# A hybrid decoder layer: attention scores of all parts one behind the other, the recurrence's 64x64 products over four quarters, normed rows turned by whole transposes

## The chip, the cores and the metric

The kernel runs on one core of one Trainium2 chip. The metric is the device time of one execution in microseconds, as the median of the runs. Before the change it is 431.32 us (three runs, 431.30 to 431.98). A core has engines that run side by side, each with its own queue of instructions in a fixed order: TensorE (PE, matrix products, with PEld for its weight loads), VectorE (DVE), ScalarE (ACT), GpSimd (POOL) and SyncE (SP, which here issues DMAs). An engine that waits for a semaphore holds up all that stands behind the waiting instruction in its queue.

## The reference

One layer of a decoder, for 256 tokens of width 1024, in float32. Two branches read the same normed input: RWKV-7 time mixing, which is a recurrence over tokens with a 64x64 state in each of 8 heads, and causal attention with 8 heads of 64. Their results are projected, gated, merged and projected again, and a gated MLP with a short convolution follows.

```python
h = rms_norm(x, norm1_g[l])
proj = h @ w_in[l]                       # one projection for both branches and the gates
...
y_a = rwkv7_time_mix(z_rwkv, ...)
...
y_b = moba_attention(q, k, v)
u_a = y_a @ w_branch_a[l]
u_b = y_b @ w_branch_b[l]
...
x = x + (g_a * u_a + g_b * u_b) @ w_out[l]
h2 = rms_norm(x, norm2_g[l])
x = x + conv_ffn(h2, w_ffn_up[l], ffn_conv_w[l], ffn_conv_b[l], w_ffn_down[l])
```

Inside the time mixing, for each head and token, then a norm over the 64 values of each head:

```python
def step(state, inp):
    r_t, w_t, k_t, v_t, a_t, b_t = inp
    sa = jnp.einsum('bhvk,bhk->bhv', state, a_t)
    state = (state * w_t[:, :, None, :] + sa[..., None] * b_t[:, :, None, :]
             + v_t[..., None] * k_t[:, :, None, :])
    return state, jnp.einsum('bhvk,bhk->bhv', state, r_t)
...
mu = jnp.mean(y, axis=-1, keepdims=True)
var = jnp.mean(jnp.square(y - mu), axis=-1, keepdims=True)
y = ((y - mu) * lax.rsqrt(var + GN_EPS)).reshape(B, S, C)
```

At this size the attention has one block of keys, so each query attends to all keys up to its own.

## The kernel before

**Weights.** Every large weight comes by DMA in pieces of 512 KB (`raw`, L221, issued on SP, four buffers), is split into a rounded part `whi` (a cast on ACT, L233) and the rest `wlo` (a subtraction on DVE, L243), and TensorE sums three products into `acc`: high by high (L271), low by high (L273), high by low (L276). L292, L293 and L296 do the same where the weight is the stationary operand. This is called the bulk here.

**Threads.** The middle of the kernel is written as generators: `chain` (the recurrence and its preparation), `bulk` (input projection, gates, the attention branch), `att` (attention) and a group norm for each chunk. Each hands back an estimate (cost, latency) with `yield`; a small loop uses the sum to choose which thread writes its next piece, so that bulk products stand between the dependent steps of the others. A scheduler then fixes the order of each engine. When the recurrence has ended, the branch of the recurrence (`branch(0)`, on `yah` and `yal`) follows, then w_out and the MLP.

**Recurrence.** The 256 tokens are cut into 4 chunks of 64. A head is given by its parity q, which is also the half of the partitions (0 to 63 or 64 to 127) that its operands lie in, and by ct (0 to 3). `pz0` (L665) is computed for all chunks ahead. Inside a chunk a triangular 64x64 matrix has to be inverted: 16x16 blocks on DVE, written to DRAM and read back into place in `X` by eight DMAs on SP (L643), then two steps on TensorE: `pp` (L711, X times the part of G below the diagonal), masked on DVE to `P` (L716), `px` (L727), added to X (L728). X has two sides, the inverse and its transpose. Then for each chunk: `pz` (L791, the state times AR; from the second chunk), added to Z (L793), `pu` (L798), copied to VU by ACT (L800) and DVE (L801), `pS` (L807) for the new state `Sn`, `pyt` in two parts that sum (L822 with the state, L826 with VU), copied to `yt`. The group norm of the chunk works on `yt` with tokens on partitions (`yc`, L758 to L767), turns it with eight 64x64 products against the identity (`pc`, L774), applies scale and bonus (`yf`, L776 and L777) and splits the result into `yah` (ACT, L778) and `yal` (DVE, L779).

**Attention.** q and k are turned (`pqk`, L876) and copied to `qkT` (ACT, L877). It has three parts: the first 128 queries with all heads, then the second 128 queries with four heads twice. For each, `scores` makes products `ps` (L893), masks or copies them into `sc` (DVE L896, ACT L899) and does the softmax (L902 to L909, exponentials on ACT), turns the weights with transposes (`ppt`, L918, copied to `pT`), and when a half of the queries is complete `weighted` makes `po` (L931), split into `ybh` (ACT, L935) and `ybl` (DVE, L936). The gates' tanh is `gt` (ACT, L955); a branch's product is merged with `gt` on DVE (L964).

PSUM has three pools: three banks `acc` for bulk, three `ch` for the recurrence, two `at` for attention.

The recurrence's loop asks for a half of the array with the operands' half of rows and of columns the same:

```python
pu = chp("pu").rearrange("p (a n) -> p a n", a=8)
for h in range(8):
    ct, q = divmod(h, 2)
    pe.matmul(pu[bsl(q), ct], X[bsl(q), 1, 4 * ct + c], Z[bsl(q), ct], start=True, stop=True)
```

Of the kernel before, what the change touches and what calls it, by code (L numbers as in the profile page):

```python
# [36 lines left out]
def body(tc, x, positions, norm1_g, w_in, rwkv_mu, w_decay_up, decay_bias, w_aaa_up,  # L37
# [5 lines left out]
    with ctx:  # L43
# [447 lines left out]
        def chain():  # L491
# [67 lines left out]
            KB = cst.tile([128, 2112], F32, name="KB")  # L559
# [45 lines left out]
            for g in range(2):  # L605
# [7 lines left out]
                for ct in (2 * g, 2 * g + 1):  # L613
                    for q in range(2):
                        dve.tensor_tensor(G[q][:, 4 * ct:4 * ct + 4], pg[ct % 2][q],
                                          gmask[:, None, :].to_broadcast([128, 4, 128]), op=OP.mult)
# [22 lines left out]
            pool.memset(X, 0.0)  # L639
            for q in range(2):  # L640
                for b in range(4):
                    q0 = bsl(q).start + 16 * b
                    nc.sync.dma_start(X[q0:q0 + 16, :, :, 16 * b:16 * b + 16],  # L643
                                      d2[4 * q + b].rearrange("x u (i n) -> i x u n", i=16))
# [15 lines left out]
            Z0 = b4("Z0", (128, 4, 4, 64))  # L660
            pz = [chp("pz0").rearrange("p (c a n) -> p c a n", c=2, a=4) for _ in range(2)]
            for c in range(4):
                for ct in range(4):
                    for q, hs in PAR:
                        pe.matmul(pz[c // 2][bsl(q), c % 2, ct], G[q][hs, 4 * ct + c, 0:64],  # L665
                                  VU[hs, c, q, ct], start=True, stop=True)
            for j in range(2):
                act.copy(Z0[:, 2 * j:2 * j + 2], pz[j])
            yield 2.5, 3.0
# [27 lines left out]
            def pair(t, g):  # L697
                return t.rearrange("p (a c) n -> p a c n", c=4)[:, :, 2 * g:2 * g + 2]


            us = [[(4 * ct + 2 * g + c, 2 * ct + c) for ct in range(4) for c in range(2)] for g in range(2)]

            def bank(nm):
                p = chp(nm)
                return p.rearrange("p (u n) -> p u n", u=8), p.rearrange("p (a c n) -> p a c n", a=4, c=2)

            def below(g):
                p, _ = bank("pp")
                for u, i in us[g]:
                    for q in range(2):  # L710
                        pe.matmul(p[bsl(q), i], G[q][bsl(q), u, 0:64], X[bsl(q), 0, u], start=True, stop=True)  # L711
# [7 lines left out]
            def onto(g, P, side):  # L719

                p, p4 = bank("px")
                for u, i in us[g]:
                    for q in range(2):
                        l, r = X[bsl(q), 1, u], P[bsl(q), i]
                        if side:
                            l, r = r, l
                        pe.matmul(p[bsl(q), i], l, r, start=True, stop=True)  # L727
                return lambda: dve.tensor_tensor(pair(X[:, side], g), pair(X[:, side], g), p4, op=OP.add)  # L728

            yield 0, 11.0  # L730
            pp = [below(g) for g in range(2)]
            P = [masked(pp[g], m16) for g in range(2)]
            yield 2.5, 3.5
            adds = [onto(0, P[0], 0), onto(1, P[1], 0), onto(0, P[0], 1)]
            for a in adds:
                a()
            yield 3.3, 4.5
            pp = [below(g) for g in range(2)]
            add = onto(1, P[1], 1)
            P = [masked(pp[g], m32) for g in range(2)]  # L740
            add()
            yield 3.3, 4.5
            for a in [onto(g, P[g], 1) for g in range(2)]:
                a()
# [6 lines left out]
            def group_norm():  # L751

                for c in range(4):
# [18 lines left out]
                    for ct in range(4):  # L772
                        for q, hs in PAR:
                            pe.matmul(p[hs, ct], yc[hs, ct], ident[hs, hs], start=True, stop=True)  # L774
# [10 lines left out]
            for c in range(4):  # L785
                Z = Z0[:, c]
                if St is not None:
                    pz = chp("pz").rearrange("p (a n) -> p a n", a=8)
                    for h in range(8):
                        ct, q = divmod(h, 2)  # L790
                        pe.matmul(pz[bsl(q), ct], AR[half(q), 4 * ct + c, 0], St[half(q), ct],  # L791
                                  start=True, stop=True)
                    dve.tensor_tensor(Z, pz[:, 0:4], Z, op=OP.add)  # L793
                    yield 0.8, 2.3
                pu = chp("pu").rearrange("p (a n) -> p a n", a=8)
                for h in range(8):
                    ct, q = divmod(h, 2)
                    pe.matmul(pu[bsl(q), ct], X[bsl(q), 1, 4 * ct + c], Z[bsl(q), ct],  # L798
                              start=True, stop=True)
# [383 lines left out]
```

## Time and profile before

| | us |
|---|---|
| median of 3 runs | 431.32 |
| the profiled execution | 431.12 |
| its span, first to last instruction | 429.0 |

The span is the time from the first to the last instruction; 2.12 us of the execution lie outside. A row of a group names line, engine, operation, out<-in, tile (rows*columns of the array), shape and count, then busy time in us and the mean of one in ns, then the idle time ahead. A row of the timeline gives start and length; a matmul's length overlaps the next one's, so what a burst costs TensorE is the distance from its start to the start of what follows. A window's row gives for each engine the busy time and the count, and the granted clock as a share of full speed.

| stage of the span | us |
|---|---|
| pz0 | 90.6 to 92.6 |
| first product on X (pp) | 117.2 |
| first scores (ps) | 123.7 |
| first pu of the recurrence | 147.9 |
| last pu of the recurrence | 183.0 |
| last weights turned (ppt), weighted (po) | 188.6, 190.5 |
| first product of the attention branch | 193.7 |
| last turned chunk (pc) | 194.1 |

### The profile page before, as it was taken

Reading aid. Unit: us, or ns where it says so; the run is one execution under the profiler, and the core shown is the slowest. Engines: PE = TensorE matmul, PEld = TensorE weight load, DVE = VectorE, ACT = ScalarE, POOL = GpSimd, SP = SyncE. Lnnn points to the kernel's source line nnn. Section 1 sums busy time; section 2 is a strip of 40 time slices with the busy share of each in tenths; the row PEclk is TensorE's granted clock in tenths of the full one; section 3 lists DMA queues with packets and bytes.
Section 4 is the critical chain, followed back from the end, with each engine's and each line's share of the span. In section 5 each row is a group of like instructions: output and inputs, shape, how many; then the busy total and the mean of one; then the engine's idle time right before and its main releaser. Section 6 shows DMA issues by size and latency. Waiting matters only on the chain.

```text
span 429.0 us, 8164 instructions
## 1 busy us (share of the span) xinstructions
PE 416.8 (97%) x3249; PEld 365.9 (85%) x3249; DVE 322.0 (75%) x553; ACT 239.1 (56%) x386; POOL 27.1 (6%) x47
## 2 busy tenths in 40 slices
PE   7799999999999999979999999999999999999996
PEld 3799989888899989969987878888888888888885
DVE  3797899779437567766786599888797797796783
ACT  6599645455345468793356466465464454464550
POOL 6920060000000000000000000000000000000000
PEclk9999999999999999989999999999999999999999
DMA  8776655563743534531665275656656656656622
GB/s 256 205 197 200 193 147 151 154 166 99 148 148 101 149 99 120 176 101 53 194 189 165 88 244 175 218 195 196 190 165 211 186 184 200 191 169 213 191 67 98
DMA packets 62404, 70.71 MB, mean 165 GB/s; under 512 B 9117, under 2 KB 52835, under 8 KB 62368
## 3 DMA queue, kind: packets, MB, share of 16 engines
q1 hardware_dynamic: 61664, 69.48, 54.3%
q0 software_dynamic: 688, 0.73, 0.6%
q8 instruction: 25, 0.41, 0.4%
q14 instruction: 11, 0.09, 0.1%
q10 hardware_dynamic: 16, 0.00, 0.0%
HBM read 68.76 MB, written 1.44 MB: 164 GB/s over the span
## 4 chain that ended last, share of the span: by engine, by line
PE 89%; ACT 4%; DVE 3%; DMA 2%; issue 1%; POOL 1%; SPq 0%; DVEq 0%; ACTq 0%; POOLq 0%
PE acc L1080 17%; PE acc L1083 8%; PE acc L271 8%; PE acc L276 8%; PE acc L273 8%; PE acc L292 4%; PE acc L293 4%; PE acc L296 4%; PE f L1099 4%; PE f L1098 4%; PE f L1100 4%; PE px L727 1%; DMA x<-in_x_dram 1%; DMA raw<-in_w_ffn_up_dram 1%; PE pp L711 1%; PE pgr L611 1%
## 5 line engine op out<-in xcount | busy, mean ns | idle before, releaser
L233 ACT CAST whi<-raw 128x1024 fp32r<-128x1024 f32 x121 | 126.7, 1051 | 124.4 <-PE acc L1080 44.9
L243 DVE TENSOR_TENSOR wlo<-raw,whi 128x1024 fp32r<-128x1024 f32 x124 | 152.2, 1230 | 50.6 <-PE acc L276 13.4
L1080 PE MATMUL acc<-hx,whi 128*128 128x512 f32 x352 | 96.7, 395 | 0.5 <-DVE bs L1088 0.5
L1080 PEld LDWEIGHTS acc<-hx,whi 128*128 128x128 f32 x352 | 60.1, 188 | 9.1 <-DVE bs L1088 1.0
L1083 PEld LDWEIGHTS acc<-hx,wlo 128*128 128x128 f32 x352 | 53.4, 188 | 7.9
L271 PE MATMUL acc<-hx,whi 128*128 128x256 f32 x232 | 58.4, 287 | 0.0
L273 PE MATMUL acc<-hx,whi 128*128 128x256 f32 x232 | 56.5, 279 | 0.0
L1083 PE MATMUL acc<-hx,wlo 128*128 128x256 f32 x352 | 54.6, 278 | 0.0
L271 PEld LDWEIGHTS acc<-hx,whi 128*128 128x128 f32 x232 | 43.7, 188 | 1.4 <-issue 0.5
L273 PEld LDWEIGHTS acc<-hx,whi 128*128 128x128 f32 x232 | 43.8, 189 | 0.4 <-issue 0.3
L276 PE MATMUL acc<-hx,wlo 128*128 128x256 f32 x232 | 36.1, 278 | 1.1 <-DVE wlo L243 1.1
L276 PEld LDWEIGHTS acc<-hx,wlo 128*128 128x128 f32 x232 | 30.9, 188 | 1.3 <-DVE wlo L243 1.3
L1099 PE MATMUL f<-whi,hb 128*128 128x512 f32 x80 | 31.2, 390 | 0.0
L1100 PE MATMUL f<-wlo,hb 128*128 128x512 f32 x80 | 31.2, 390 | 0.0
L1098 PE MATMUL f<-whi,hb 128*128 128x512 f32 x80 | 31.2, 389 | 0.0
L1088 DVE TENSOR_REDUCE an<-acc 128x256 f32<-128x512 f32 x22 | 15.2, 689 | 7.2 <-PE acc L1083 6.3
L292 PE MATMUL acc<-whi,hx 128*128 128x512 f32 x48 | 19.3, 402 | 0.0
L293 PE MATMUL acc<-whi,hx 128*128 128x512 f32 x48 | 18.8, 392 | 0.0
L1100 PEld LDWEIGHTS f<-wlo,hb 128*128 128x128 f32 x80 | 15.0, 188 | 3.2
L1098 PEld LDWEIGHTS f<-whi,hb 128*128 128x128 f32 x80 | 15.0, 188 | 2.8
L1099 PEld LDWEIGHTS f<-whi,hb 128*128 128x128 f32 x80 | 15.0, 188 | 2.7
L296 PE MATMUL acc<-wlo,hx 128*128 128x512 f32 x48 | 14.9, 392 | 0.0
(294 smaller groups left out, 650.5 us busy)
## 6 DMA issues: line engine op xcount, KB each, us to landing
raw<-in_w_ffn_up_dram SPq DMA_DIRECT2D x44, 512.0 KB, 4.5
raw<-in_w_in_dram SPq DMA_DIRECT2D x42, 512.0 KB, 4.6
raw<-in_w_ffn_down_dram SPq DMA_DIRECT2D x22, 512.0 KB, 4.1
raw<-in_w_out_dram SPq DMA_DIRECT2D x8, 512.0 KB, 3.7
x<-in_x_dram SPq DMA_DIRECT2D x8, 256.0 KB, 3.4
raw<-in_w_branch_b_dram SPq DMA_DIRECT2D x4, 512.0 KB, 4.3
raw<-in_w_branch_a_dram SPq DMA_DIRECT2D x4, 512.0 KB, 4.0
out_dram<-o SPq DMA_DIRECT2D x3, 256.0 KB, 2.0
```

The costliest lines, as they stand in the source:

```text
L233: act.copy(hi[:, :k * c], raw[:, :k * c])
L243: eng.tensor_tensor(lo[:, :n], raw[:, :n], hi[:, :n].bitcast(F32), op=OP.subtract)
L271: pe.matmul(om, wh[:, k, ms], xh[:, k0 + k], start=k0 + k + m == 0, stop=False, skip_group_check=True)
L273: pe.matmul(om, wh[:, k, ms], xl[:, k0 + k], start=False, stop=False, skip_group_check=True)
L276: pe.matmul(om, wl[:, k, ms], xh[:, k0 + k], start=False, stop=k0 + k == nk - 1 and m == n - 1, skip_group_check=True)
L292: pe.matmul(ps_[t], xh[:, K, ts], wh[:, k], start=K == 0, stop=False)
L293: pe.matmul(ps_[t], xl[:, K, ts], wh[:, k], start=False, stop=False)
L1080: pe.matmul(ps_[m], wh[:, k, ms], hx[:, k0 + k].rearrange("p a s -> p (a s)"), start=k0 + k == 0, stop=False, skip_group_check=True)
L1083: pe.matmul(ps_[m][:, 0:S], wl[:, k, ms], hh[:, k0 + k], start=False, stop=k0 + k == 7, skip_group_check=True)
L1098: pe.matmul(fin[f], hb[:, 0, i, ts], wh[:, 0, cs], start=st, stop=False)
L1099: pe.matmul(fin[f], hb[:, 1, i, ts], wh[:, 0, cs], start=False, stop=False)
L1100: pe.matmul(fin[f], hb[:, 0, i, ts], wl[:, 0, cs], start=False, stop=False)
```

## The change

1. Attention: the scores and the softmax of all three parts are written first, then the transposes and weighted products of all. For this the parts keep buffers of their own: `sc0`, and `sc1` in the place of `KB`, which is no longer read then.
2. The 64x64 products of pz0, pp, px, pz, pu and pyt are written in an order `QA` over two parities, so that they fall on all four quarters (half of rows, half of columns) of the array. Rows go by one parity and columns by the other, so each step writes two PSUM banks, one for each, in place of one; the copies behind it become twice as many with half the size. G's slots and Z0's layout follow. The transposed side of px (`turned_`) stays on two quarters.
3. `pc`: two transposes of 128x128 for a chunk in place of eight 64x64 products.
4. X is read back by more DMAs: eight for side 0 on SP, then sixteen for side 1, eight on SP and eight on POOL.
5. The estimates in `yield` change with it.

In the program as it is scheduled, three places are shown. In the first burst of `pp` (L724 now), all eight products on G of one parity stand ahead of the eight of the other; from there on they alternate in the order of QA.

ScalarE's queue around the copies `qkT` of the turned q and k, ahead of the first softmax, before:

```order
L842 COPY qkv<-acc 128x512
L877 COPY qkT_1521<-pqk 128x512 x2
L955 ACTIVATE gt<-acc 128x512
L877 COPY qkT_1564<-pqk 128x512 x2
L233 CAST whi<-raw 128x1024 x3
L906 ACTIVATE sc,sm<-sc,mx 128x128 x8
```

and now:

```order
L875 COPY qkv<-acc 128x512
L910 COPY qkT_1537<-pqk 128x512 x2
L233 CAST whi<-raw 128x1024
L910 COPY qkT_1580<-pqk 128x512
L1002 ACTIVATE gt<-acc 128x512
L233 CAST whi<-raw 128x1024
L910 COPY qkT_1580<-pqk 128x512
L233 CAST whi<-raw 128x1024
L943 ACTIVATE sc,sm<-sc,mx 128x128 x8
```

Two of the three casts of weights, which need their raw piece from DRAM, now stand between the copies.

TensorE's queue where the recurrence ends, before (pyt is that of the last chunk, pc turns the last chunk, L271 and L273 on ybh and ybl are the attention branch):

```order
L826 MATMUL pyt<-VU,G_784 64x64
L826 MATMUL pyt<-VU,G_785 64x64
L918 MATMUL ppt<-ident,sc 128x128 x8
L931 MATMUL po<-pT,qkv 64x128 x16
L271 MATMUL acc<-ybh,whi 128x256 x2
L774 MATMUL pc<-ident,yc 64x64 x8
L273 MATMUL acc<-ybl,whi 128x256
L271 MATMUL acc<-ybh,whi 128x256
```

and now at the last pc:

```order
L273 MATMUL acc<-ybl,whi 128x256
L276 MATMUL acc<-ybh,wlo 128x256 x4
L798 MATMUL pc<-ident,yc 128x128 x2
L271 MATMUL acc<-yah,whi 128x256 x3
L273 MATMUL acc<-yal,whi 128x256
L271 MATMUL acc<-yah,whi 128x256
L273 MATMUL acc<-yal,whi 128x256
```

The last transposes and weighted products of attention have moved ahead of the recurrence's last chunks, the attention branch stands ahead of the last pc, and the recurrence's branch (on yah and yal) directly behind it.

VectorE's queue at the same place, before:

```order
L767 TENSOR_TENSOR yc<-yc,st 128x256
L936 TENSOR_TENSOR ybl<-po,ybh 128x4x128
L776 TENSOR_TENSOR yf<-pc,A_1335 128x256
L777 TENSOR_TENSOR yf<-yf,zr 128x256
L779 TENSOR_TENSOR yal<-yf,yah 128x4x64
L964 SCALAR_TENSOR_TENSOR gt<-gt,acc 128x512
L243 TENSOR_TENSOR wlo<-raw,whi 128x1024
```

and now:

```order
L792 TENSOR_TENSOR yc<-yc,st 128x256
L1011 SCALAR_TENSOR_TENSOR gt<-gt,acc 128x512
L243 TENSOR_TENSOR wlo<-raw,whi 128x1024
L1011 SCALAR_TENSOR_TENSOR gt<-gt,acc 128x512
L801 TENSOR_TENSOR yf<-pc,A_1351 128x256
L243 TENSOR_TENSOR wlo<-raw,whi 128x1024
L802 TENSOR_TENSOR yf<-yf,zr 128x256
L804 TENSOR_TENSOR yal<-yf,yah 128x4x64
L1011 SCALAR_TENSOR_TENSOR gt<-gt,acc 128x512
```

The gates' merge and a split of weights now stand ahead of and between the two operations on the last chunk.

The diff, cut to its core:

```diff
+        QA = ((0, 0), (1, 1), (0, 1), (1, 0))
+        def gslot(ct, c=0):
+            return 8 * (ct % 2) + 4 * (ct // 2) + c
...
-            KB = cst.tile([128, 2112], F32, name="KB")
+            KB = cst.tile([128, 2112], F32, name="KB", tag="KB")
...
+            def to_x(eng, side, x, us_, src):
+                b = src[1]
+                q0 = bsl(side).start + 16 * b
+                eng.dma_start(X[q0:q0 + 16, x, us_, 16 * b:16 * b + 16],
+                              d2[4 * src[0] + b, x, src[2]].rearrange("u (i n) -> i u n", i=16))
             for q in range(2):
                 for b in range(4):
-                    q0 = bsl(q).start + 16 * b
-                    nc.sync.dma_start(X[q0:q0 + 16, :, :, 16 * b:16 * b + 16],
-                                      d2[4 * q + b].rearrange("x u (i n) -> i x u n", i=16))
+                    to_x(nc.sync, q, 0, slice(0, 16), (q, b, slice(0, 16)))
+            for q in range(2):
+                for b in range(4):
+                    for a in range(2):
+                        to_x((nc.sync, nc.gpsimd)[a], a, 1, slice(8 * q, 8 * q + 8), (q, b, slice(8 * a, 8 * a + 8)))
...
             for c in range(4):
-                for ct in range(4):
-                    for q, hs in PAR:
-                        pe.matmul(pz[c // 2][bsl(q), c % 2, ct], G[q][hs, 4 * ct + c, 0:64],
-                                  VU[hs, c, q, ct], start=True, stop=True)
+                for j in range(2):
+                    for q, a in QA:
+                        ct = 2 * j + a
+                        pe.matmul(pz[q][bsl(a), c, j], G[q][half(q), gslot(ct, c), 0:64],
+                                  VU[half(q), c, q, ct], start=True, stop=True)
...
+            def below():
+                p = [bank("pp") for _ in range(2)]
+                for i in range(8):
+                    for q, a in QA:
+                        u = 8 * a + i
+                        pe.matmul(p[q][bsl(a), i], G[q][bsl(q), u, 0:64], X[bsl(q), 0, u], start=True, stop=True)
                 return p
...
+            def plain(P):
+                p = [bank("px") for _ in range(2)]
+                for i in range(8):
+                    for q, a in QA:
+                        pe.matmul(p[a][bsl(q), i], X[bsl(a), 1, 8 * q + i], P[q][bsl(a), i], start=True, stop=True)
+                return p
+            def turned_(q, P):
+                p = bank("px")
+                for i in range(8):
+                    for a in range(2):
+                        pe.matmul(p[bsl(a), i], P[bsl(a), i], X[bsl(a), 1, 8 * q + i], start=True, stop=True)
+                return p
...
                     p = chp("pc").rearrange("p (a n) -> p a n", a=8)
-                    for ct in range(4):
-                        for q, hs in PAR:
-                            pe.matmul(p[hs, ct], yc[hs, ct], ident[hs, hs], start=True, stop=True)
+                    for j in range(2):
+                        pe.transpose(p[:, 2 * j:2 * j + 2].rearrange("p a n -> p (a n)"),
+                                     yc[:, 2 * j:2 * j + 2].rearrange("p q n -> p (q n)"), ident)
...
+                    pz = two("pz")
+                    for j in range(2):
+                        for q, a in QA:
+                            ct = 2 * j + a
+                            pe.matmul(pz[q][bsl(a), j], AR[half(q), 4 * ct + c, 0], St[half(q), ct],
+                                      start=True, stop=True)
+                    for q in range(2):
+                        dve.tensor_tensor(Z0[:, q, c], pz[q][:, 0:2], Z0[:, q, c], op=OP.add)
+                    yield 0.5, 2.3
+                pu = two("pu")
+                for j in range(2):
+                    for q, a in QA:
+                        pe.matmul(pu[a][bsl(q), j], X[bsl(a), 1, 8 * q + 4 * j + c], Z0[bsl(a), q, c, j],
                                   start=True, stop=True)
-                act.copy(VU[bsl(0), c, 0], pu[bsl(0), 0:4])
-                dve.tensor_copy(VU[bsl(1), c, 1], pu[bsl(1), 0:4])
-                yield 0.9, 2.3
+                for a in range(2):
+                    act.copy(VU[bsl(0), c, 0, a:4:2], pu[a][bsl(0), 0:2])
+                    dve.tensor_copy(VU[bsl(1), c, 1, a:4:2], pu[a][bsl(1), 0:2])
+                yield 0.6, 2.3
...
+                py = two("pyt")
...
+            sc0 = b4("sc", (128, 8, 128))
+            sc1 = cst.tile([128, 2112], F32, name="sc1", tag="KB")[:, 0:2048].rearrange("p (h k) -> p h k", k=256)
+            parts = ((0, 0, 8, sc0), (1, 0, 4, sc1[:, 0:4]), (1, 1, 4, sc1[:, 4:8]))
...
-            p0 = yield from scores(0, 0, 8)
-            yield weighted(0, p0)
-            pa = yield from scores(1, 0, 4)
-            pb = yield from scores(1, 1, 4)
-            yield weighted(1, pa + pb)
-            yield 0, 2.5
+            for i, part in enumerate(parts):
+                scores(*part)
+                yield 0.9, 3.0
+                softmax(*part)
+            yield 0, 4.0
...
+            p0 = turned_w(*parts[0])
+            yield 0.9, 2.5
+            weighted(0, p0)
+            pa = turned_w(*parts[1])
+            yield 1.8, 3.0
+            pb = turned_w(*parts[2])
+            yield 0.9, 2.5
+            weighted(1, pa + pb)
+            yield 1.9, 2.5
```

More of the change, by code (lines that the diff above doesn't have):

```diff
@@ L659, in chain @@
             yield 2.5, 4.0
[L660 to L661 removed]
+            Z0 = b4("Z0", (128, 2, 4, 2, 64))
+            pz = [chp("pz0").rearrange("p (c j n) -> p c j n", c=4, j=2) for _ in range(2)]
             for c in range(4):
[L663 to L669 removed]
+                for j in range(2):
[4 more added lines that the diff above has]
+            for q in range(2):
+                act.copy(Z0[:, q], pz[q])
+            yield 1.4, 3.0
             bp = zr
@@ L695, in chain @@
             A2 = bon
-            def pair(t, g):
-                return t.rearrange("p (a c) n -> p a c n", c=4)[:, :, 2 * g:2 * g + 2]
-            us = [[(4 * ct + 2 * g + c, 2 * ct + c) for ct in range(4) for c in range(2)] for g in range(2)]
             def bank(nm):
[L704 to L711, printed above, removed]
+                return chp(nm).rearrange("p (u n) -> p u n", u=8)
+            def below():
[4 more added lines that the diff above has]
+                        pe.matmul(p[q][bsl(a), i], G[q][bsl(q), u, 0:64], X[bsl(q), 0, u], start=True, stop=True)
                 return p
@@ L717, in masked @@
                 return P
[L719 to L728, printed above, removed]
-            yield 0, 11.0
@@ L731, in chain, with added @@
[L731 to L744, printed above, removed]
+            def added(side, g, p):
+                v = X[:, side, 8 * g:8 * g + 8]
+                dve.tensor_tensor(v, v, p, op=OP.add)
@@ new lines, in chain @@
+            yield 0, 11.0
+            pp = below()
+            P = [masked(pp[q], m16) for q in range(2)]
+            yield 1.4, 3.5
+            px = plain(P)
+            pt = turned_(0, P[0])
+            for a in range(2):
+                added(0, a, px[a])
+            added(1, 0, pt)
+            yield 2.4, 4.5
+            pp = below()
+            pt = turned_(1, P[1])
+            P = [masked(pp[q], m32) for q in range(2)]
+            added(1, 1, pt)
+            yield 2.4, 4.5
+            pt = [turned_(q, P[q]) for q in range(2)]
@@ L745, in chain @@
+            for q in range(2):
+                added(1, q, pt[q])
             yield 2.3, 4.0
@@ L815, in chain @@
                         dve.tensor_tensor(Sn, Sn, pcb, op=OP.mult)
-                py = chp("pyt").rearrange("p (a n) -> p a n", a=8)
+                py = two("pyt")
                 if St is not None:
-                    for h in range(8):
-                        ct, q = divmod(h, 2)
-                        hs = half(q)
-                        pe.matmul(py[hs, ct], AR[hs, 4 * ct + c, 1], St[hs, ct], start=ct == 0,
-                                  stop=False, skip_group_check=True)
-                for h in range(8):
-                    ct, q = divmod(h, 2)
-                    pe.matmul(py[half(q), ct], G[q][:, 4 * ct + c, 64:128], VU[:, c, q, ct],
-                              start=St is None and ct == 0, stop=ct == 3, skip_group_check=True)
+                    for j in range(2):
+                        for q, a in QA:
+                            ct = 2 * j + a
+                            pe.matmul(py[q][half(a), j], AR[half(q), 4 * ct + c, 1], St[half(q), ct],
+                                      start=j == 0, stop=False, skip_group_check=True)
+                for j in range(2):
+                    for q, a in QA:
+                        ct = 2 * j + a
+                        pe.matmul(py[q][half(a), j], G[q][:, gslot(ct, c), 64:128], VU[:, c, q, ct],
+                                  start=St is None and j == 0, stop=j == 1, skip_group_check=True)
                 ny[c] = t1("yt", (128, 4, 64))
-                act.copy(ny[c], py[:, 0:4])
-                yield 1.9, 2.0
+                for q in range(2):
+                    act.copy(ny[c][:, q:4:2], py[q][:, 0:2])
+                yield 1.5, 2.0
                 if c < 3:
@@ L899, in scores, with softmax @@
                         act.copy(sc[:, q:nh:2, 0:128], pq[q][:, :, 0:128])
-                yield 2.1, 2.5
+            def softmax(t, j, nh, sc):
+                nk = 128 * (t + 1)
                 mx = sb.tile([128, nh], F32, name="mx", tag="mx", bufs=2)
@@ L920, in scores @@
                     pTs.append(pT)
-                yield 0.9, 2.5
                 return pTs
```

28 lines of the change are left out of this document (9 added, 19 removed).

## The prediction

> **What bounds the kernel now.** I began with the page of the profile: the span, the busy shares, the clock row and the shares of the chain.
>
> ```profile
> span 429.0 us, 8164 instructions
> ...
> PE 416.8 (97%) x3249; PEld 365.9 (85%) x3249; DVE 322.0 (75%) x553; ACT 239.1 (56%) x386; POOL 27.1 (6%) x47
> ...
> PEclk9999999999999999989999999999999999999999
> ...
> PE 89%; ACT 4%; DVE 3%; DMA 2%; issue 1%; POOL 1%; SPq 0%; DVEq 0%; ACTq 0%; POOLq 0%
> ```
>
> TensorE is busy for 97% and carries 89% of the chain that ends last. So time is won in two ways only: fewer microseconds of products, or less idle TensorE. DVE and ACT matter where TensorE stops for them. The clock row has one slice below 9, the 19th (193 to 204 us), so I took the waits of TensorE and then windows there.
>
> ```profile
> PE ppt L918 <- DVE sc L909: 1.9, 1, 1.9
> ...
> PE pc L774 <- DVE yc L767: 0.8, 1, 0.8
> ...
> PE acc L271 <- ACT ybh L935: 0.7, 1, 0.7
> ```
>
> ```profile
> 184.00:194.70 10.70, 7.37 (x96) 6.17 (x92) 6.14 (x15) 8.67 (x20) 0.00 (x0) 0.84 0.31 98
> 188.20:191.70 3.50, 3.12 (x20) 2.80 (x22) 2.43 (x8) 2.63 (x6) 0.00 (x0) 0.51 0.12 44
> ```
>
> These three waits (us in total, times, longest) lie in the 10.7 us of the first window (length, busy PE, PEld, DVE, ACT, POOL, then clock): TensorE works 7.37 of them, and for 3.5 us the granted clock is 0.51. The timeline says why.
>
> ```profile
> 183.01 0.68 PE L798 MATMUL pu<-Z,X 64*64 64x64 f32 x16
> ...
> 188.57 1.97 PE L918 MATMUL ppt<-ident,sc 128*128 128x128 f32 x8 [1.88 <-DVE sc L909]
> 190.47 2.52 PE L931 MATMUL po<-pT,qkv 128*64 128x128 f32 x32
> ...
> 194.12 0.68 PE L774 MATMUL pc<-ident,yc 64*64 64x64 f32 x16
> 194.73 0.39 PE L273 MATMUL acc<-ybl,whi 128*128 128x256 f32 x1
> ```
>
> By 183 us no product of the input projection is left to fill with. The last softmax ends late, its transposes wait, and the attention branch (L271 on ybh) can't start before 193.7.
>
> **The change, part by part.** The sum is made against the profiled execution: 431.12 us, its span of 429.0 and 2.12 around it; the median of the runs is 0.20 above that.
>
> *Products in four quarters.* First the price of one pass (the trace shows each f32 product as two).
>
> ```profile
> 90.61 2.08 PE L665 MATMUL pz<-VU,G 64*64 64x64 f32 x64
> 92.62 0.39 PE L271 MATMUL acc<-hx,whi 128*128 128x256 f32 x1
> ...
> 117.22 0.44 PE L711 MATMUL pp<-X,G 64*64 64x64 f32 x4
> 117.59 0.66 PE L876 MATMUL pqk<-ident,qkv 128*128 128x128 f32 x4
> ...
> 163.26 0.68 PE L822 MATMUL pyt<-Sn,AR 64*64 64x64 f32 x16
> 163.87 0.69 PE L826 MATMUL pyt<-VU,G 128*64 128x64 f32 x16
> 164.48 0.68 PE L774 MATMUL pc<-ident,yc 64*64 64x64 f32 x16
> ```
>
> From start to next start, 64 passes on two quarters take 2.01 us and 16 take 0.61. That is 0.14 to begin and 29.2 ns a pass. The four passes at 117.22 all stand in one quarter: (0.37 - 0.14)/4 = 58 ns. Two quarters at once thus halve the price. That the L826 products, which share all 128 rows and differ by their half of the columns, also take 0.61 for 16 says that sharing rows need not cost. Four at once is not in the trace. I bound it: below, 14.6 ns (halved again); above, 58 (no overlap); I take 14.6, as doubling the quarters once gave all of it, with 29.2 as the nearest row against it. The passes:
>
> ```profile
> L711 PE MATMUL pp<-X,G 64*64 64x64 f32 x128 | 4.6, 220 | 0.0
> ...
> L727 PE MATMUL px<-P,X 64*64 64x64 f32 x64 | 2.1, 220 | 0.0
> L791 PE MATMUL pz<-Sn,AR 64*64 64x64 f32 x48 | 2.0, 224 | 0.0
> ```
>
> In four quarters stand: 64 of pz0 (the 90.61 row), 96 of the 128 of pp (in its first burst the scheduler puts the eight products of one parity's G ahead of the other's, so 32 passes stay in two), 64 of px with the plain side, and in the recurrence 48 of pz, 64 of pu and 48 of pyt with the state. The other px, pS and pyt on VU keep their price. 384 passes x 14.6 ns = **-5.6 us**.
>
> [...]
>
> *pc as two transposes.* Prices of transposes, and of the weighted products for the next part:
>
> ```profile
> 119.48 0.60 PE L876 MATMUL pqk<-ident,qkv 128*128 128x128 f32 x4
> 119.83 0.36 PE L271 MATMUL acc<-hx,whi 128*128 128x256 f32 x1
> ...
> 153.22 1.05 PE L931 MATMUL po<-pT,qkv 128*64 128x128 f32 x16
> 154.19 0.39 PE L271 MATMUL acc<-hx,whi 128*128 128x256 f32 x1
> ```
>
> Four transposes take 0.35 us with their beginning, so two take some 0.25 in place of 0.61: four chunks x 0.36 = **-1.4** (bounds 0.26 and 0.44 a chunk).
>
> *Attention's scores first.* From 183.01 to 194.73 run five bursts of 16 passes (pu, two pyt, two pc: 5 x 0.61), eight transposes (2 x 0.35), 32 passes of po (2 x 0.97) and two first products of the branch (0.24): 5.9 us of work in 11.72. In the new order all scores and softmax stand ahead of the recurrence, with bulk between the transposes of each part, and the attention branch fills the recurrence's end (TensorE's rows above). So the wait for sc, the half clock and the wait for ybh go: **-5.8** (bounds -4 and -5.8). Gross: -12.8.
>
> *What it adds, first: SP and the scores.*
>
> ```profile
> 110.55 4.04 SPq L643 DMA_DIRECT2D X<-d  x8
> 114.69 4.32 SPq L221 DMA_DIRECT2D raw<-in_w_in_dram  x4
> ...
> DMA to landing us min/median/max: 2.0/2.3/2.9
> ...
> raw<-in_w_in_dram SPq DMA_DIRECT2D x42, 512.0 KB, 4.6
> ...
> 122.94 2.01 ACT L233 CAST whi<-raw 128x1024 fp32r<-128x1024 f32 x2
> ...
> 123.65 0.48 PE L893 MATMUL ps<-qkT,qkT 64*128 64x128 f32 x2
> ```
>
> An X DMA takes SP 0.505 us. Eight more push the raw loads by 4.0: the first is issued at 118.7 and lands 4.6 later, at 123.3. ACT now has a cast of such a raw, gt's tanh and a second cast ahead of the last qkT copy (ACT's rows above): 123.3 + 1.0 = 124.3, a copy and tanh to 125.4, the second cast (the raw behind lands at 124.4) to 126.4, the copy to 126.9. TensorE reaches ps at 123.65 - 0.93 (pz0) - 0.37 (four passes) + 1.54 (pp) + 2 x 1.07 (px) = 126.0, or 126.2 with the wait that follows. So a new wait of **+0.7** (bounds 0 and 2, when the second raw lands a microsecond later). The other eight DMAs go through POOL, which has nothing else to do there, and only side 1 waits for them: nothing. Side 0: the last of its eight is issued at 114.1, done on SP at 114.6 and lands 2.0 to 2.9 after its issue, by 117.0; TensorE is there 0.9 earlier than the 117.22 of before: **+0.25** (bounds 0 and 0.7).
>
> *Second: the last pc.* In the new order the last pc stands directly ahead of the recurrence branch's first product; of before, 94 bulk products of the attention branch stood between.
>
> ```profile
> 193.68 0.68 DVE L936 TENSOR_TENSOR ybl<-po,ybh 128x512 fp32r<-128x512 f32 x1
> 194.85 0.42 DVE L776 TENSOR_TENSOR yf<-pc,A 128x256 f32<-128x256 f32 x1 [0.48 <-PE pc L774]
> 195.31 0.42 DVE L777 TENSOR_TENSOR yf<-yf,zr 128x256 f32<-128x256 f32 x1
> ...
> 197.79 0.69 DVE L964 SCALAR_TENSOR_TENSOR gt<-gt,acc 128x512 f32<-128x512 f32 x1 [1.16 <-PE acc L276]
> 198.40 1.22 DVE L243 TENSOR_TENSOR wlo<-raw,whi 128x1024 fp32r<-128x1024 f32 x1
> ...
> 195.76 0.41 ACT L778 CAST yah<-yf 128x256 fp32r<-128x256 f32 x1 [2.13 <-DVE yf L777]
> ```
>
> TensorE waits for yah (ACT), and that for DVE, whose row is gt, yf, wlo, yf. From pc's end: the rest of a gt (0.12 + 0.69 - 0.25 = 0.55), yf 0.46, wlo 1.22, yf 0.46, yah 0.45: **+3.1** (bounds 1.5, if gt and wlo get by before, and 3.4, if gt starts with pc's end). Queued behind: all of the branch, then xt. Third: the VU and yt copies come in twice as many, smaller pieces, one of them behind a ybl (0.68): **+0.2** (bounds 0 and 0.7); the bulk products after pu hide the others, and cost up to 0.4 a chunk where that cover is missing.
>
> Costs 0.7 + 0.25 + 3.1 + 0.2 = 4.25. Sum: -12.8 + 4.25 = -8.55, so 431.12 - 8.55 = **422.6 us** (span 420.5).
>
> **Rivals.** *R1, quarters give little:* the passes are issued at 22 to 29 ns whatever quarter they have; for it, that no stretch of before has an interval per 64-column pass below 29.2; against it, that 58 became 29. At 29.2 the 5.6 goes, and with TensorE late the waits at ps and X (0.95) too: 422.6 + 5.6 - 0.95 = 427.2; at 22 (half of the gain) 425.4 with both waits left. So 425.4 to 427.2.
>
> *R2, the wait for yah takes the place of the one for sc:* it is 3.1 us of idle TensorE in one piece, and the 3.5 us at 0.51 of before stand right behind such idle time. The branch would then run 3.5 us at half clock: +1.7, with the upper 3.4 of the wait 424.6, with every cost at its upper bound (2 + 0.7 + 0.7) 427. About 425. Against it: the 1.9 of before came with 0.8 and other gaps shortly ahead, here TensorE is full ahead of pc. [...]
>
> *R3, slower: passes that share rows with a running one are held back.* The order puts quarters (0,1) and (1,0) behind (0,0) and (1,1). If a load into a half of the rows must wait for a running pass there, each runs alone at 58: 384 x 28.8 = +11.1 on the 427.2 of R1, 438.3. It decides from 3.9/384 = 10 ns above 29.2, that is 39 ns a pass. Against it stand the L826 row and the 0.61 for 16 there. [...]
>
> *R4, the gap stays:* the recurrence, with fewer products, waits for its own copies, and the end is as late: 431.12 - 2.75 = 428.4 and up. Against it: bulk stands between all its steps.
>
> **How the numbers follow.** Forecast 0.50 (own range 420 to 425), R1 0.24, R2 0.13, R3 0.08, R4 0.05. The low end is the forecast with yah's wait at its lower bound and no wait at ps: 422.6 - 1.6 - 0.7 = 420.3, with the remaining 0.45 of small waits 419.8; I say 419.7. The high end takes in R1 and R2 and R4's near end, 428.4. Left out are R3, half of R4 and the forecast's tails. About 0.2% (0.86 us) is what a measurement of this kernel can tell from no change. Faster: all but R3 and most of R4, 0.88; same 0.04; slower 0.08.
>
> **What would show it.** For quarters: 64 passes of pz0 and of plain px in 1.1 us from start to next start (2.0 if R1, near 3.8 if R3). For pc: 0.25. For the gap: no wait of ppt for sc, no row at 0.51 near 184 to 195, branch products between the last bursts. For the costs: a wait of ps for the qkT copy near 126 of 0.7, one of acc for yah of 3.1 near 193, the recurrence's branch done some 9 us earlier than before. Wrong would be: a rate above 22, a wait at yah beyond 4 or a clock below 0.9 behind it, or new waits of pu, pz and pS on the smaller copies.

## The result, and the profile after

The changed kernel takes 424.85 us (median of 4 runs, 422.93 to 425.50) against 431.31 for the kernel before. The ratio is 0.9842, with a 95% interval of 0.9819 to 0.9864: 6.5 us faster, where 8.7 were forecast against the median (8.55 against the profiled execution, which went from 431.12 to 425.09, that is 6.03). The time is inside the range, 2.2 above the forecast. The savings came as forecast, 12.6 us of 12.8; of the costs, three did not come at all, and others came that had no term.

Here are lines from the page of the changed kernel: its span, busy shares, clock row and shares of the chain:

```profile
span 422.9 us, 8098 instructions
...
PE 408.6 (97%) x3193; PEld 358.2 (85%) x3193; DVE 322.0 (76%) x560; ACT 239.2 (57%) x394; POOL 31.3 (7%) x55
...
PEclk9999999999999999998999999999999999999999
...
PE 81%; DVE 8%; ACT 4%; DMA 4%; issue 2%; POOL 1%; SPq 0%; DVEq 0%; ACTq 0%; POOLq 0%
```

TensorE has 8.2 us less work and the same share of the span. One slice of the clock row is still below 9, now the 19th of 40 (190 to 201 us); in the kernel before it was the 18th (182 to 193 us), not the 19th as the prediction read it, which touches none of its sums. The waits of TensorE in the changed kernel name what stands there now:

```profile
PE acc L271 <- ACT yah L803: 2.8, 1, 2.8
...
PE ppt L956 <- ACT pT L957: 0.9, 1, 0.9
```

The three waits of before (1.9, 0.8 and 0.7) are gone. The timeline of TensorE in the changed kernel, at the places that the prediction named:

```profile
89.88 1.16 PE L682 MATMUL pz<-VU,G 64*64 64x64 f32 x64
90.97 0.39 PE L271 MATMUL acc<-hx,whi 128*128 128x256 f32 x1
...
116.00 1.44 PE L724 MATMUL pp<-X,G 64*64 64x64 f32 x64
117.37 0.66 PE L909 MATMUL pqk<-ident,qkv 128*128 128x128 f32 x4
...
125.74 1.16 PE L928 MATMUL ps<-qkT,qkT 64*128 64x128 f32 x16
129.77 1.16 PE L724 MATMUL pp<-X,G 64*64 64x64 f32 x64
130.75 1.10 PE L749 MATMUL px<-X,P 64*64 64x64 f32 x32
...
160.51 0.46 PE L852 MATMUL pyt<-Sn,AR 64*64 64x64 f32 x16
160.90 0.69 PE L857 MATMUL pyt<-VU,G 128*64 128x64 f32 x16
161.52 0.44 PE L798 MATMUL pc<-ident,yc 128*128 128x128 f32 x2
161.79 1.04 PE L956 MATMUL ppt<-ident,sc 128*128 128x128 f32 x8
...
194.42 0.38 PE L798 MATMUL pc<-ident,yc 128*128 128x128 f32 x2
197.59 0.62 PE L271 MATMUL acc<-yah,whi 128*128 128x256 f32 x3 [2.80 <-ACT yah L803]
```

From start to next start, 64 passes of pz0 take 1.09 us (2.01 before), 16 passes of pyt 0.39 (0.61), and a pc 0.27 (0.61). That is 0.16 to begin and 14.6 ns a pass. The scores (125.74) begin without a wait. In the last two rows TensorE has two transposes, and then nothing until yah is there. VectorE and ScalarE in that stretch, from the timeline of the changed kernel:

```profile
194.62 0.69 DVE L1011 SCALAR_TENSOR_TENSOR gt<-gt,acc 128x512 f32<-128x512 f32 x1 [1.06 <-PE acc L276]
195.22 0.42 DVE L801 TENSOR_TENSOR yf<-pc,A 128x256 f32<-128x256 f32 x1
195.55 1.21 DVE L243 TENSOR_TENSOR wlo<-raw,whi 128x1024 fp32r<-128x1024 f32 x1
196.69 0.42 DVE L802 TENSOR_TENSOR yf<-yf,zr 128x256 f32<-128x256 f32 x1
...
197.14 0.40 ACT L803 CAST yah<-yf 128x256 fp32r<-128x256 f32 x1 [1.92 <-DVE yf L802]
```

The reader sees a chain of five steps, two of which (gt and wlo, 0.69 and 1.21 us) have nothing to do with yah and only stand ahead in the queue: pc has ended at 194.80, and yf begins at 195.22, behind gt. Windows of the changed kernel, the wait and the stretch behind it (length, busy PE, PEld, DVE, ACT, POOL, clock, DMA share, GB/s):

```profile
194.70:197.60 2.90, 0.10 (x2) 0.01 (x1) 2.43 (x5) 0.93 (x2) 0.00 (x0) 1.00 0.61 176
198.67:202.08 3.41, 3.41 (x19) 3.41 (x18) 0.00 (x0) 0.00 (x1) 0.00 (x0) 0.50 0.32 119
```

In this trace the clock is halved about one microsecond after TensorE starts again, for 3.41 us. Products of the branch that take 0.12 us each take 0.21 there; together that costs 1.5 us.

### The profile page after: what moved, and what is told of

Read it like the earlier page. It is cut to its first block, busy times and chain, and to the rows that moved or that the text cites. A ratio compares the mean times of both kernels' runs of the same rounds, so it can differ in the third digit from the quotient of the medians.

```text
span 422.9 us, 8098 instructions
## 1 busy us (share of the span) xinstructions
PE 408.6 (97%) x3193; PEld 358.2 (85%) x3193; DVE 322.0 (76%) x560; ACT 239.2 (57%) x394; POOL 31.3 (7%) x55
## 4 chain that ended last, share of the span: by engine, by line
PE 81%; DVE 8%; ACT 4%; DMA 4%; issue 2%; POOL 1%; SPq 0%; DVEq 0%; ACTq 0%; POOLq 0%
PE acc L1127 17%; PE acc L1130 9%; PE acc L271 7%; PE acc L276 7%; PE acc L273 6%; PE f L1146 4%; PE f L1147 4%; PE f L1145 4%; PE acc L292 4%; PE acc L296 4%; PE acc L293 4%; DVE wlo L243 2%; ACT sc L943 1%; DMA x<-in_x_dram 1%; DMA raw<-in_w_ffn_up_dram 1%
## 5 line engine op out<-in xcount | busy, mean ns | idle before, releaser
L271 PE MATMUL acc<-hx,whi 128*128 128x256 f32 x232 | 58.7, 288 | 0.0
L273 PE MATMUL acc<-hx,whi 128*128 128x256 f32 x232 | 56.7, 280 | 0.0
L271 PEld LDWEIGHTS acc<-hx,whi 128*128 128x128 f32 x232 | 43.7, 188 | 1.6 <-issue 0.7
L273 PEld LDWEIGHTS acc<-hx,whi 128*128 128x128 f32 x232 | 43.8, 189 | 0.4 <-issue 0.3
```

What stands on the lines that cost most here:

```text
L271: pe.matmul(om, wh[:, k, ms], xh[:, k0 + k], start=k0 + k + m == 0, stop=False, skip_group_check=True)
L273: pe.matmul(om, wh[:, k, ms], xl[:, k0 + k], start=False, stop=False, skip_group_check=True)
```

## The experiments

All times are medians beside the kernel before in the same batch (431.76 in the first, 430.82 in the second). Where a few tenths matter, I compare the *stage* in the traces: from the first product of pz0 to the first product of w_out (`acc<-whi,mh`). It is 127.02 us before and 120.94 in the changed kernel, and 121.56 in the second trace of the changed kernel (experiment 1), so a difference of less than 0.6 us needs a row of its own to show it. Outside the stage the traces of before and after differ too: the changed one reaches pz0 0.73 us earlier and takes 0.72 longer behind the stage. Of the latter, 0.5 lies behind the last product, where the three traces with the products of before (before, 4 and 6) take 3.65 us to the end and the seven others 4.14 or 4.15. That cost goes with the part of the change that is not attention; the prediction has no term for it, and its cause was not looked for.

**1. The changed kernel again**, unedited, as a base.

> The changed kernel once more, as the base for the runs beside it. If the half clock behind the wait for yah is what parts its runs (423 to 425.5 us), then runs near 423 show a mean granted clock of 1.0 and runs near 425 show 0.996, as 3.7 us at half clock are 1.85 of 423. If the spread has another source (the start of the program, the loads), clock and time go their own ways. Median 424.9, within 1.

Measured: 424.78 (422.92 to 426.64, 6 runs), ratio 0.9844 (0.9812 to 0.9876); the profile shows the same wait of 2.8 and the same half clock. Of its six runs, two have a mean clock of 1.0 (422.92 and 425.31) and four 0.996 (423.20 to 426.64). So the half clock comes in some runs and not in others, and it isn't the only source of the spread: the start is another. The same instruction, with the same instructions ahead of it in its queue, in the kernel before

```profile
21.41 1.19 PE L276 MATMUL acc<-hx,wlo 128*128 128x256 f32 x8 [1.15 <-DVE wlo L243]
```

and in the changed one

```profile
20.82 1.19 PE L276 MATMUL acc<-hx,wlo 128*128 128x256 f32 x8 [0.21 <-DVE wlo L243]
```

waits 1.15 us or 0.21. Over all ten profiles of this case the wait is either 0.15 to 0.22 or 1.15 to 1.19, five times each, whatever was edited far behind it. So single profiled executions differ by a microsecond ahead of the first changed instruction, and the stage is the better measure.

**2. The last pc earlier.** The estimate ahead of it, for the last chunk only:

```diff
-                    yield 0, 6.0
+                    yield 0, (6.0 if c < 3 else 2.0)
```

> The last pc is written some 17 products before the end of the attention branch (the latency estimate ahead of it 2 instead of 6 for the last chunk), nothing else. Theory A (the wait for yah and the half clock behind it cost what the trace shows): the 2.8 us of wait and the 1.5 us lost at half clock go, TensorE waits 0.3 us for yc instead; 4.0 below the changed kernel, 420.9, all runs at clock 1.0. Rival B (the wait only moves to the yal, wlo or gt behind): within 1 of the changed kernel. Rival C (the half clock is not caused by the wait): only the wait goes, 422.3, clock still 0.996.

Measured: 420.56 (419.97 to 421.33), ratio 0.9753 (0.9728 to 0.9777), 4.2 below the base. The timeline of TensorE in this kernel:

```profile
191.21 0.41 PE L798 MATMUL pc<-ident,yc 128*128 128x128 f32 x2
191.37 0.36 PE L273 MATMUL acc<-ybl,whi 128*128 128x256 f32 x1
...
194.20 0.40 PE L271 MATMUL acc<-yah,whi 128*128 128x256 f32 x2
```

No wait for yah is left in its list. Between pc and the first product that needs its result now stand 2.8 us of the attention branch. The stage is 116.53, 4.4 shorter. The pc stands 23 products earlier (the expectation's 17 was too few). Theory A holds, B falls, and C falls too: the traced run's mean clock is 0.999, and one of its six runs shows less than that (0.994; it was not traced). This kernel is also the fastest of the study, with that of experiment 7.

**3. Products in pairs of quarters.** Same buffers and copies; each burst runs through two quarters first and then through the other two. The edit at pp, the others alike:

```diff
+        QP = (QA[:2], QA[2:])
...
-                for i in range(8):
-                    for q, a in QA:
+                for i, q, a in [(i, q, a) for pr in QP for i in range(8) for q, a in pr]:
```

> The changed kernel with each burst of 64x64 products in another order: first all products of quarters (0,0) and (1,1), then all of (0,1) and (1,0); same buffers, same copies. Theory A (what saves time is that four quarters run at once): 64 passes of pz0 take 2.0 us again instead of 1.09, 16 passes of pz 0.61 instead of 0.39, and 384 passes x 14.6 ns = 5.6 come back: 430.5, within 1. Rival B (the gain came from elsewhere, the smaller copies or the order of the steps): within 1 of the changed kernel.

Measured: 426.24 (425.46 to 426.76), ratio 0.988 (0.985 to 0.9911), so only 1.5 above the base. The timeline of this kernel:

```profile
90.10 1.91 PE L681 MATMUL pz<-VU,G 64*64 64x64 f32 x64
91.94 0.39 PE L271 MATMUL acc<-hx,whi 128*128 128x256 f32 x1
...
147.82 0.47 PE L822 MATMUL pu<-Z,X 64*64 64x64 f32 x16
```

The long bursts went back as theory A said: pz0 takes 1.84, and in the stage pz0, pp and plain px together take 3.3 us more (pp alone 2.0, where one burst had also fallen into runs of a single quarter). The short bursts did not: pu, pz and pyt stay within 0.05 us of the changed kernel, for three or four bursts each together (pu 1.62 for four bursts, 0.40 each, where 0.61 was expected). That the second pair of quarters begins before the first has drained is my estimate, from these 0.40 us and the size of the seams in experiment 8; no row shows it. My figure of 5.6 for this edit was therefore wrong, and the edit undoes only the long bursts. It also moved ACT's work so that the wait for pT (0.9) is gone, and its traced run has the wait for yah of 2.8 without the half clock, so the run time doesn't measure the quarters. The passes do. That the wait for yah had no half clock behind it here is taken up below, at the account of the half clock.

**4. Attention alone**, in the kernel before:

```diff
-            p0 = yield from scores(0, 0, 8)
-            yield weighted(0, p0)
-            pa = yield from scores(1, 0, 4)
-            pb = yield from scores(1, 1, 4)
-            yield weighted(1, pa + pb)
+            for i, part in enumerate(parts):
+                scores(*part)
+                yield 0.9, 3.0
+                softmax(*part)
+            yield 0, 4.0
...
```

> The kernel before with the attention part of the change alone (scores and softmax first). Theory A (the gap of before goes, but its loss comes back at the last pc, at the half clock behind it, and in smaller waits): no wait of ppt for sc, a wait for yah of 2.8 us or more, half clock behind it; 431 to 432, no gain. Rival B (the terms of the prediction: the gap of 5.8 goes, 3.1 + 0.2 come back): 428.6, clock 1.0.

Measured: 428.86 (427.49 to 431.63, 10 runs), ratio 0.9953 (0.9929 to 0.9976). The waits of this kernel hold one at the place:

```profile
PE acc L271 <- ACT yah L778: 2.4, 1, 2.4
```

It is B in the time: the terms of the prediction were about right here, and A's sum, made from the one trace of the changed kernel, was 2 to 3 us too high. In part that is the half clock, which that trace has and this one has not. In this kernel five of ten runs have a mean clock of 1.0 (427.49 to 428.90), the others 0.99 to 0.996 (428.82 to 431.63); so B's clock of 1.0 holds in half of the runs only.

**5. The other half alone:** the changed kernel with the attention of before (the edit of 4 the other way round).

> The changed kernel with the attention part as it was before; quarters, pc and the X loads stay as changed. Theory A (the product savings of 5.7 and 1.6 read from the traces are worth their full sum, whatever the attention does): 431.6 - 7.3 = 424.3, within 1.2, with the wait of ppt for sc and the half clock of before, and no wait for yah. Rival B (with fewer products TensorE only arrives earlier at a softmax that ends no earlier, since its steps hang on ACT and DVE): the wait for sc grows by what was saved, 428 or more.

Measured: 426.83 (426.04 to 427.62), ratio 0.9906 (0.9882 to 0.9931): 4.0 us instead of 7.3. Its waits and a window over the end of the recurrence:

```profile
PE pyt L857 <- ACT VU L830: 2.0, 1, 2.0
PE ppt L953 <- DVE sc L944: 1.5, 1, 1.5
```

```profile
176.00:190.20 14.20, 9.98 (x109) 8.54 (x107) 8.84 (x23) 11.67 (x26) 0.00 (x0) 0.76 0.34 109
```

The products are as cheap as in the changed kernel, but 3.3 us of what they save is lost again, most of it in one place. TensorE comes earlier to the end of the recurrence, has no bulk left, waits for VU and then for sc, and in 14.2 us has a mean clock of 0.76, which is 3.4 us lost (before, 10.7 us at 0.84, 1.7). Neither theory had it whole: A's sum doesn't hold alone, B's 428 is too much.

**6. Attention alone, with the last pc earlier** (edits 4 and 2 on the kernel before).

> The kernel before with the attention part alone, and the last pc moved ahead in the same way. Theory A (attention's order is worth the gap, and only the last pc's place gave half of it back): the 2.4 us of wait go, and the half clock that four or five of ten runs had behind it: 428.9 - 2.4 - 0.7 = 425.8, all runs at clock 1.0. Rival B (the old 64x64 products at pc hide the wait elsewhere): 428.9.

Measured: 425.73 (425.65 to 427.04), ratio 0.9888 (0.9863 to 0.9912). The trace has no wait of TensorE in the stage. Theory A holds: once the last pc stands earlier, the attention's order is worth 5.1 us instead of 2.9.

**7. One table load less ahead of pT**, on top of 2; in the first chunk's group norm:

```diff
-                    yield 0, 1.0
+                    yield 0, (1.0 if c else 3.0)
```

> The kernel with the last pc moved ahead, and in the first chunk's group norm the square root written later (latency 3 instead of 1), so that ScalarE does gt's tanh before it loads the table of the square root: one table load of 1.28 us less stands ahead of the copies pT. Theory A (the wait of 0.9 us of ppt for pT comes from the two table loads): the wait goes, 419.7. Rival B (ScalarE is late there anyway): 420.6, with the wait at 0.9.

ScalarE ahead of the copy pT in the changed kernel, with two loads of a function's table (L790 is the square root, L1002 gt's tanh):

```profile
153.06 1.28 ACT L790 ACT_TABLE_LOAD   x1
...
154.67 1.28 ACT L1002 ACT_TABLE_LOAD   x1
...
156.93 0.60 ACT L957 COPY pT<-ppt 128x512 f32<-128x512 f32 x1
```

Measured: 420.86 (419.00 to 422.19, 6 runs), ratio 0.9764 (0.9735 to 0.9792), where A expected 419.7. The wait in this kernel's list:

```profile
PE ppt L956 <- ACT pT L957: 0.3, 1, 0.3
```

One of the two loads is gone from this place, the wait shrinks from 0.9 to 0.3, and the stage goes from 116.53 to 115.79. So the table load made two thirds of the wait, where A had all of it; the time of the whole doesn't show the gain, within the spread of the start. The loads alone don't make a wait: the traces of experiments 3, 4 and 6 have the same two loads ahead of pT and no wait. TensorE is later there: the products pu ahead of these transposes begin at 158.30 in experiment 3, just as the second load ends (158.38), and in the changed kernel a microsecond before its end (154.97 against 155.95).

**8. The orders of quarters**, one profiled run:

```diff
+        QR = ((0, 0), (0, 1), (1, 0), (1, 1))
+        QC = ((0, 0), (1, 0), (0, 1), (1, 1))
...
-                for i in range(8):
-                    for q, a in QA:
+                for i, q, a in [(i, q, a) for q, a in QA for i in range(8)]:
                         pe.matmul(p[a][bsl(q), i], X[bsl(a), 1, 8 * q + i], P[q][bsl(a), i], start=True, stop=True)
```

(QR in place of QA at pz0, QC at pp, the loop shown at plain px.)

> The changed kernel with three orders of quarters, for the price of a pass: pz0 with neighbours that share rows, (0,0), (0,1), (1,0), (1,1); pp with neighbours that share columns; plain px with eight products of one quarter after the other. Theory A (each quarter works through its own passes at 58 ns and only products of the same quarter hold each other up): pz0 64 passes in 1.09 us as in the changed kernel, second pp 0.98, px 64 passes near 3.7 us, less where the next quarter begins early. Rival B (a load waits for a running pass in the same rows): pz0 2 us or more.

The timeline of this kernel (427.53 us):

```profile
90.90 1.16 PE L684 MATMUL pz<-VU,G 64*64 64x64 f32 x64
91.99 0.39 PE L271 MATMUL acc<-hx,whi 128*128 128x256 f32 x1
...
122.46 3.23 PE L742 MATMUL px<-P,X 64*64 64x64 f32 x61
...
132.55 1.16 PE L726 MATMUL pp<-X,G 64*64 64x64 f32 x64
133.53 1.11 PE L750 MATMUL px<-X,P 64*64 64x64 f32 x32
```

Neighbours that share rows: 1.09 for 64 passes, the same as in the changed kernel. Neighbours that share columns: 0.98, the same. One quarter after the other: about 3.1, against 3.7 for 64 passes at 58 ns; so each of the three seams saves some 0.2, an estimate from these two numbers. A holds in these times, B falls. Such a seam of 0.2 would also account for experiment 3's short bursts: 0.14 + 16 x 29.2 ns = 0.61 without it, 0.40 measured.

## Why the prediction was right, and where its sum was off

The terms, from the traces of before and of the changed kernel (the stage, sums over each kind of product):

| term | forecast | measured |
|---|---|---|
| quarters | -5.6 | -5.7 (pz0 0.9, pp 1.9, px 0.8, pz 0.7, pu 0.8, pyt 0.7) |
| pc | -1.4 | -1.6 |
| gap at the end of attention | -5.8 | -5.3 (idle 3.3; ppt, po and ps, partly at half clock, 1.9) |
| ps behind the qkT copies | +0.7 | 0 |
| X, side 0 | +0.25 | 0 |
| wait for yah | +3.1 | +2.8 |
| smaller copies (VU, yt) | +0.2 | 0 |
| waits for pT and pg | none | +1.1 (0.9 and 0.2) |
| half clock behind yah | none (rival R2) | +1.5 |
| bulk cut into more bursts | none | +1.0 |
| all else | none | +0.2 |
| sum of the stage | -8.55 | -6.1 |

- **Quarters.** The forecast took 14.6 ns a pass, and the rows of pz0 and pyt give 14.6; the second burst of pp, 64 passes in 0.98 us with its beginning, is no dearer. R1, with its 22 to 29 ns, did not come: 64 passes of 64 columns take 1.09 us, 17 ns each with the beginning counted in. R3 did not come either, and experiment 8 tested it directly: neighbours that share rows take the same 1.09 us.
- **The gap.** It went as forecast, and its price was nearly right (5.3 of 5.8): experiment 6, which has no cost at pc, gains 5.1.
- **The wait for yah.** The forecast's chain was gt, yf, wlo, yf, yah, 3.14 us; the trace shows the same five in the same order and 2.8. Experiment 2 confirms the place.
- **Half clock.** This is the largest part that was off. The text set the wait beside the row with 0.51, and still gave the halving 0.13 as a rival (R2), since TensorE is full ahead of this pc and not ahead of the other. That reason failed: four traces have this wait of 2.8 us, and three of them (the changed kernel, experiments 1 and 8) a mean clock of 0.996, as have four of the six runs of experiment 1. In the changed kernel the stretch at half clock is longer than the wait, 3.41 us.

  Experiment 3 is the trace with the same wait and a clock of 1.0. In the traces of the changed kernel and of before, every change of the clock lies a whole number of times 3.413 us behind the moment of the first full clock: 57, 58 and 123 times in the changed kernel (first full clock 4.11 us into the span), 53, 54 and 124 times before (7.33 us). In experiment 3 the first full clock comes at 4.47. Counted from the first full clock in pieces of that length, here are the piece ahead of the halving and the halved one in the changed kernel, then the two pieces that the wait falls in in experiment 3:

```profile
195.25:198.66 3.41, 1.06 (x8) 1.02 (x9) 2.28 (x5) 0.40 (x1) 0.00 (x0) 1.00 0.52 169
198.67:202.08 3.41, 3.41 (x19) 3.41 (x18) 0.00 (x0) 0.00 (x1) 0.00 (x0) 0.50 0.32 119
```

```profile
195.62:199.03 3.41, 1.71 (x15) 1.47 (x13) 2.35 (x4) 1.05 (x1) 0.00 (x0) 1.00 0.66 211
199.03:202.44 3.41, 2.32 (x18) 2.27 (x19) 1.03 (x3) 0.40 (x1) 0.00 (x0) 1.00 0.54 162
```

  In the changed kernel most of the wait lies in one piece, in which TensorE is busy for 1.06 of 3.41 us. In experiment 3 the wait, which ends at 200.1, is cut at 199.03; TensorE is busy for 1.71 us of the one piece and 2.32 of the other, and neither is followed by a halving. The piece ahead of the halving of before has 1.77 busy us, so the busy time alone does not part them. That the wait's place among these pieces decides is an estimate from these three traces, and no run tested it; it would fit a half clock that comes in some runs and not in others, as the first full clock comes at another time in each of the three. Of the ten runs of the changed kernel on record, six have a mean clock of 0.996 and average 425.0 us, four have 0.999 or 1.0 and average 423.9. A fair forecast would have carried about half to two thirds of 1.5 in the sum.
- **ps and X.** In the step "Eight more push the raw loads by 4.0: the first is issued at 118.7" the push was right and the time was not. SP's queue in the changed kernel, then ScalarE:

```profile
109.11 7.85 SPq L651 DMA_DIRECT2D X<-d  x16
117.06 6.69 SPq L221 DMA_DIRECT2D raw<-in_w_in_dram  x5
...
121.05 1.05 ACT L233 CAST whi<-raw 128x1024 fp32r<-128x1024 f32 x1 [0.57 <-DMA raw<-in_w_in_dram]
...
125.00 0.58 ACT L910 COPY qkT<-pqk 128x512 f32<-128x512 f32 x1
```

  Sixteen X loads took SP 7.85 us, 3.8 more than the eight of before. But they began 1.4 us earlier (109.11 against 110.55): the forecast moved TensorE forward by what pz0 saves and left SP at the times of before. So the raw load was issued at 117.06, and its cast began at 121.05 instead of 123.3. The last qkT copy ends at 125.6, the scores begin at 125.74: no wait, with 0.1 us to spare. Side 0 of X cost nothing either; in experiment 1 the other side, priced at nothing, held plain px up for 0.4. That neither cost came is in part luck, a matter of tenths.
- **Smaller copies, pT and bulk.** No wait of pu, pz or pS for the smaller copies came. The wait for pT had no term: it hangs on two table loads of ScalarE (the square root of the first chunk's norm, then tanh) and on how early TensorE is there (experiment 7). And each time TensorE went from bulk to another burst and back cost some 0.2 us here (the first bulk product takes on average 0.22 instead of 0.115, the last 0.19); the new order has 22 such returns in the stage instead of 19, which is 0.5 of the 1.0. Most of the rest lies in the bulk products themselves: between 165 and 185 us they follow each other in 0.116 to 0.118 us, in the trace of before in 0.113. Why was not settled.
- **R4** did not come in the changed kernel, but it is what happens without the attention's part: experiment 5 loses 3.3 of 7.3 us at the recurrence's end.

In short: the savings came by the mechanisms named, and the wait for yah as well. In the profiled run, what stood behind that wait was rival R2 and not the forecast: a clock below 0.9 there was one of the prediction's own signs of being wrong, and R2's 424.6 lies nearer to the measured time than 422.6. Of the costs, those that did not come (0.7, 0.25 and 0.2) hide a part of those that had no term (1.5, 1.1 and 1.0); so it is partly luck that the time is only 2.2 off. The recurrence's branch ended 6.8 us earlier, at 210.97 instead of 217.79, where some 9 were forecast.

## What to carry to other kernels

When a gap on the busiest engine is closed by moving work ahead of it, look at what now stands last before the next dependent stage, and price the queue in front of each step of its chain: here an attention order worth 5 us gave 2 to 3 of them back until the last turned chunk was moved 23 products earlier. A saving in products is worth the more, the more other work there is to move up behind it: the same 7.3 us gave 4.0 without the attention's order, and some 6.1 with it (experiment 2's 11.2 less experiment 6's 5.1). And where an idle stretch is no shorter than one behind which the trace has shown a halved clock (here 2.8 us against the 1.9 of before), a good half of that loss belongs in the sum and not only in a rival.

## What the runs showed of the hardware

- In 64x64 products, f32 passes over four quarters of the array took 14.6 ns each (changed kernel: 64 of pz0 in 1.09 us, 16 of pyt in 0.39), over two 29.2 (before: 2.01 and 0.61), in one 58, an estimate (before: four of pp in 0.37, less the 0.14 to begin of the two longer bursts). The three orders tried over four quarters cost the same: 1.09 us for 64 passes of pz0 in two of them, 0.98 for pp in two. One quarter after the other, 64 passes of px took 3.1 us in experiment 8, 0.6 less than 64 times 58 ns, which is some 0.2 for each seam, an estimate. In two phases of a pair each, 16 passes of pu took 0.40 us in experiment 3, in the usual order 0.39.
- In the traces of before and of the changed kernel, every change of TensorE's clock lies a whole number of times 3.413 us behind the first full clock (53, 54 and 124; 57, 58 and 123). In the changed kernel a wait of 2.8 us was followed by 3.41 us at half clock, worth 1.5 us; of the four traces with this wait three have a mean clock of 0.996, and experiment 3, where the wait lies across two such pieces, has 1.0. The halving began 0.3 us ahead of TensorE's restart in the kernel before (188.24 against 188.57) and 1.1 us after it in the changed one (198.67 against 197.59).
- A load of ScalarE's tables took 1.28 us, each of 14 times in the trace of before and in that of the changed kernel. Going from bulk products to another burst and back cost TensorE some 0.2 us in the changed kernel (the first bulk product 0.22 us and the last 0.19, in place of 0.115).
- Ahead of any edit, one wait near 21 us took 0.2 or 1.2 us with the same instructions (0.15 to 0.22 in five of the ten profiles, 1.15 to 1.19 in five).
